# The down projection of a decoder layer as seven products of quarters, with sums kept in DRAM

## The chip, the cores and the metric

The kernel runs on one core of one Trainium2 chip. The metric is the device time of one execution in microseconds; the number reported is the median of several runs. A core has the tensor engine (PE, with its weight loads shown apart as PEld), the vector engine (DVE), the scalar engine (ACT), GpSimd (POOL), and the sync engine (SP), whose queue issues every DMA of this kernel. Each engine takes its own instructions in the order in which the program wrote them, and waits at an instruction until what it needs is there.

## What is computed

One layer of a hybrid decoder: a mixing block, a layer norm, a SwiGLU block and a second layer norm, in float32. The change lies in the SwiGLU block and what follows it:

```python
def swiglu(h, w_ffn_in, w_ffn_out):
    gate, up = jnp.split(jnp.einsum('bld,df->blf', h, w_ffn_in), 2, axis=-1)
    return jnp.einsum('blf,fd->bld', jax.nn.silu(gate) * up, w_ffn_out)

xp = layernorm(ALPHA * xp + swiglu(xp, ...), ln2_g, ln2_b)
```

There are 1024 prompt tokens and 32 sample tokens, 1056 in all; the model is 1024 wide, and the hidden layer is 2816 wide, which is 22 tiles of 128 (`NF`).

## The kernel before

Activations are kept transposed: the features lie on the 128 partitions, the tokens run along the row. A float32 product is made of three matmuls. Each operand is split into a high half in a short float format (a copy by ACT) and the remainder (a subtraction by DVE); the three are high by high, high by low and low by high. The splits of weights are lines L183 and L184 in `Weights.split`, those of activation rows L1751 and L1752 in `split`. A weight piece is a page of up to four 128x128 blocks; up to eight raw pieces (`NRAW`) are loaded and up to four (`NSPLIT`) are split ahead of the one in use.

The order on the engines comes from the way the program is written out. The main line writes the matmuls, and between groups of them it calls `unit()`, which splits the next weight piece (`W.step()`) and then lets spawned generators (`layernorm`, `hidden` and the like) write a piece of their work (`pump`). Rows live in pages of 128x544 from three pools of 18, 19 and 45; when a page is taken, POOL writes one column of it (L254), and that memset waits until the page's last user is done. `take` takes a page, `give` returns it; `spare(n)` asks whether n are free.

**Gate and up** (`for f in range(NF)`, 22 turns) already are computed as seven products of quarters: the two inputs halves by gate and up on the weights' side, the two halves of the tokens (512 and 544) by the two halves of the input on the other. A turn has the products A11·B11, A12·B21, S2·T2, S3·T3, A22·T4, S1·T1 and S4·B22; POOL makes the sums S1 to S4 of the weights for each turn (L1677 to L1688), and the sums T of the activations were made once before. For f below 12 (`NE`), A11 and A12 are made earlier, and their results are stored and loaded again (`recall`). At the end of a turn the products silu(gate)·up of both halves of the tokens are stored to DRAM: L2002 for the first half, and L2025 for the second, after the product of L2023.

**Down projection and second norm.** The tokens go in three groups, `GT`: 272, 512 and 272. For each group `hidden(g)` loads the 22 tiles of hidden rows from DRAM and splits them. For each of the 8 output tiles of 128 features, 22 inputs by 3 matmuls add up in one PSUM bank:

```python
mm(ps, wh[:, f % 4, :], xh, start=(f == 0), stop=False)
mm(ps, wh[:, f % 4, :], xl, start=False, stop=False)
mm(ps, wl[:, f % 4, :], xh, start=False, stop=(f == NF - 1))
```

These are L2125 to L2127, 1056 of 272 columns and 528 of 512. The weights are loaded and split anew for each group, 144 pieces. DVE adds the bank to the residual, the first norm's output from DRAM (L2134), and POOL adds up the sum over tiles for the mean (L2136). The norm of a group is a generator which is written between the matmuls of the next group. It subtracts the mean, squares, adds up, makes 1/sqrt by an estimate of ACT and a Newton step of DVE, and multiplies. The last group has its own form, `Last`: most of the mean and of the squares is made while the last tiles are still under way (`center`, L2066 to L2071), and `finish` (L2073 to L2109) corrects this by the last tile and writes the result.

Of the kernel before, what the change touches and what calls it, by code (L numbers as in the profile page):

```python
# [91 lines left out]
GT = [(0, 272), (272, 784), (784, 1056)]  # L92
# [8 lines left out]
HLAG = 3  # L101


class Weights:
# [4 lines left out]
    def __init__(self, k):  # L109
# [5 lines left out]
        self.keep, self.again = {}, {}  # L115

    def raw(self, ap, uses=1):
        self.src.append(ap)
        self.uses.append(uses)
        return len(self.src) - 1  # L120
# [32 lines left out]
    def load(self, upto=1 << 30):  # L153
        while self.loaded < min(upto, len(self.src)) and self.live < NRAW:
            ap = self.src[self.loaded]
            t = self.k.wp.tile([P, 512], F32, tag="wr", bufs=NRAW, name=f"wr{self.loaded}")[:, :ap.shape[1]]
            self.k.nc.sync.dma_start(out=t, in_=ap)
            self.tile[self.loaded] = t
            self.loaded += 1
            self.live += 1  # L160

# [10 lines left out]
    def split(self):  # L172
# [7 lines left out]
        hi, lo = (k.wp.tile([P, 512], F32R, tag=t, bufs=NSPLIT, name=f"{t}{i}")[:, :w] for t in ("wh", "wl"))  # L180
# [53 lines left out]
def _program(k):  # L234
# [1425 lines left out]
    hd = [k.dp.tile([P, T], F32, name=f"hd{f}") for f in range(NF)]  # L1660
# [56 lines left out]
    wfo = I["w_ffo_t"]  # L1717
    fo = {(g, d): W.whole(wfo[:, d * NF * P:(d + 1) * NF * P]) for g in range(len(GT)) for d in range(8)}

# [160 lines left out]
    def hidden(g):  # L1880

        t0, t1 = GT[g]
        w = t1 - t0
        raws = []
        for f in range(NF + HLAG):
            if f < NF:
                yield from wait(("h", f))
                while not spare(3 if ("h", NF - 2) in flags else 11):
                    yield BLOCK
                r = take([P, w], F32, f"hr{g}_{f}")  # L1890
                dma(out=r, in_=hd[f][:, t0:t1])
                raws.append(r)
                if w < 300:
                    x = take([P, HW_], F32R, f"hx{g}_{f}")
                    HL[g, f] = x[:, 0:w], x[:, 272:272 + w]
                else:
                    HL[g, f] = tuple(take([P, w], F32R, f"h{x}{g}_{f}") for x in "xy")
            if f >= HLAG:
                split(*HL[g, f - HLAG], raws[f - HLAG])
                give(f"hr{g}_{f - HLAG}")  # L1900
                flags.add(("hl", g, f - HLAG))
                if f % 2:
                    yield 0.0

    def rows(g):

        t0, t1 = GT[g]
        while not spare(8):
# [330 lines left out]
```

## Time and profile before

| | |
|---|---|
| three runs | 1274.58, 1272.57, 1274.81 us; median 1274.58 |
| the profiled execution | 1276.04 us, span 1274.3 us |
| mean granted clock of the tensor engine | 0.992 |
| moved by DMA | 221.23 MB, mean 174 GB/s |

The runs time the whole execution. The span reaches from the first to the last instruction of the profiled one. In rows of busy time the number behind an x is the count of instructions. "a, b" behind a bar are the busy time in us of the group and the mean of one in ns, and behind a second bar stand the idle time just ahead and what ended it. In rows of waits the three numbers are the total in us, the count and the longest. In a timeline, the first two numbers are start and duration in us. A span of a matmul in such rows overlaps that of its neighbours.

### The profile page before, as it was taken

The page shows a single profiled execution, that of the slowest core. Times are in us where ns is not written, and L with a number is a line of the kernel's source. Part 1 is how long each engine was busy: PE and PEld are TensorE (multiplying, and loading weights), DVE is VectorE, ACT ScalarE, POOL GpSimd, SP SyncE. Part 2 cuts the span into 40 slices and gives each one's busy share as a digit, 9 for nine tenths or more (in the row PEclk, how much of TensorE's full clock was granted, in tenths as well). Part 3 has the DMA queues.
Part 4 walks back from the last instruction along what each step waited for, and adds up shares of the span by engine and source line. Part 5 has one row for each costly group of instructions (what it writes and reads, how often), then busy time and mean ns, then how long its engine had stood idle before and what let it go on. Part 6 is the DMA issues. An engine that isn't in the chain of part 4 may idle for free.

```text
span 1274.3 us, 25095 instructions
## 1 busy us (share of the span) xinstructions
PE 1242.6 (98%) x8679; PEld 1125.3 (88%) x8679; DVE 822.3 (65%) x1845; ACT 585.1 (46%) x1310; POOL 376.6 (30%) x1201
## 2 busy tenths in 40 slices
PE   9999999989999999998999999999999999999996
PEld 7887789989899889986999999889999899888996
DVE  6697974676675675778566566655655775533786
ACT  7674743755646432686222222222423554422664
POOL 1007511206631144515433442233232112111220
PEclk9999999999999999998999999999999999999998
DMA  9986563455435877565544433342323886533671
GB/s 342 311 278 217 170 223 88 154 172 150 124 108 185 293 240 228 182 194 187 166 149 138 151 128 119 107 134 84 108 88 109 272 286 192 162 93 100 206 242 63
DMA packets 146751, 221.23 MB, mean 174 GB/s; under 512 B 23344, under 2 KB 53168, under 8 KB 146608
## 3 DMA queue, kind: packets, MB, share of 16 engines
q1 hardware_dynamic: 146624, 219.63, 53.9%
q8 instruction: 68, 1.11, 0.4%
q14 instruction: 59, 0.48, 0.1%
HBM read 156.30 MB, written 64.29 MB: 173 GB/s over the span
## 4 chain that ended last, share of the span: by engine, by line
PE 58%; DVE 2%; DMA 2%; ACT 1%; issue 1%; POOL 0%; SPq 0%; DVEq 0%; ACTq 0%; POOLq 0%
PE acc L2127 6%; PE acc L1863 6%; PE acc L2125 6%; PE acc L2126 6%; PE acc L1865 6%; PE acc L1864 6%; PE ms L1863 5%; PE ms L1865 5%; PE ms L1864 5%; PE acc L460 2%; PE acc L459 2%; PE acc L458 2%; DMA hr<-hd 1%; PE ms L1459 1%; ACT mx L1584 0%
## 5 line engine op out<-in xcount | busy, mean ns | idle before, releaser
L184 DVE TENSOR_TENSOR wl<-wr,wh 128x512 fp32r<-128x512 f32 (+1 forms) x270 | 191.8, 712 | 116.0 <-ACT wh L183 103.5
L183 ACT CAST wh<-wr 128x512 fp32r<-128x512 f32 (+1 forms) x270 | 161.2, 600 | 225.9 <-PE acc L2126 97.0
L458 PE MATMUL acc<-xh,wh 128*128 128x272 f32 (+1 forms) x528 | 174.8, 331 | 0.0
L460 PE MATMUL acc<-xh,wl 128*128 128x272 f32 (+1 forms) x528 | 174.5, 331 | 0.0
L2127 PE MATMUL acc<-hx,wl 128*128 128x272 f32 (+1 forms) x528 | 171.7, 325 | 2.0 <-DVE wl L184 1.9
L459 PE MATMUL acc<-xl,wh 128*128 128x272 f32 (+1 forms) x528 | 172.3, 327 | 0.1
L2125 PE MATMUL acc<-hx,wh 128*128 128x272 f32 (+1 forms) x528 | 171.3, 324 | 0.2 <-ACT wh L183 0.2
L183 ACT CAST wh<-S 128x512 fp32r<-128x512 f32 x88 | 54.6, 620 | 176.1 <-PE acc L1864 105.9
L2127 PEld LDWEIGHTS acc<-hx,wl 128*128 128x128 f32 x528 | 99.3, 188 | 11.7 <-DVE wl L184 3.8
L458 PEld LDWEIGHTS acc<-xh,wh 128*128 128x128 f32 x528 | 100.7, 191 | 7.8 <-issue 1.2
L459 PEld LDWEIGHTS acc<-xl,wh 128*128 128x128 f32 x528 | 100.4, 190 | 7.8 <-issue 0.8
L2125 PEld LDWEIGHTS acc<-hx,wh 128*128 128x128 f32 x528 | 99.2, 188 | 8.7 <-issue 0.5
L460 PEld LDWEIGHTS acc<-xh,wl 128*128 128x128 f32 x528 | 100.5, 190 | 6.9 <-issue 0.2
L2126 PE MATMUL acc<-hx,wh 128*128 128x272 f32 x352 | 101.3, 288 | 0.2 <-DVE hx L1752 0.2
L184 DVE TENSOR_TENSOR wl<-S,wh 128x512 fp32r<-128x512 f32 x88 | 72.7, 826 | 39.1 <-ACT wh L183 37.3
L2126 PE MATMUL acc<-hy,wh 128*128 128x512 f32 x176 | 69.2, 393 | 0.0
L2126 PEld LDWEIGHTS acc<-hx,wh 128*128 128x128 f32 x352 | 66.3, 188 | 0.7 <-DVE hx L1752 0.5
L460 PE MATMUL acc<-mh,wl 128*128 128x272 f32 (+1 forms) x192 | 62.8, 328 | 0.0
L458 PE MATMUL acc<-mh,wh 128*128 128x272 f32 (+1 forms) x192 | 62.2, 326 | 0.0
L459 PE MATMUL acc<-ml,wh 128*128 128x272 f32 (+1 forms) x192 | 62.1, 324 | 0.0
L1863 PE MATMUL ms<-T2h,wh 128*128 128x272 f32 x176 | 50.8, 290 | 4.0 <-ACT wh L183 4.0
L2136 POOL TENSOR_TENSOR s<-y,s 128x272 f32<-128x272 f32 (+1 forms) x17 | 22.5, 1324 | 102.1 <-DVE y L2134 102.0
(649 smaller groups left out, 3439.3 us busy)
## 6 DMA issues: line engine op xcount, KB each, us to landing
wr<-in_w_ffo_t SPq DMA_DIRECT2D x120, 256.0 KB, 2.8
wr<-in_w_ffi_t SPq DMA_DIRECT2D x112, 256.0 KB, 2.7
wkh<-wh SPq DMA_DIRECT2D x60, 256.0 KB, 4.3
wkl<-wl SPq DMA_DIRECT2D x60, 256.0 KB, 4.1
wh<-wkh SPq DMA_DIRECT2D x60, 256.0 KB, 3.2
wl<-wkl SPq DMA_DIRECT2D x60, 256.0 KB, 3.6
wr<-in_w_in_t SPq DMA_DIRECT2D x44, 256.0 KB, 5.3
hd<-x SPq DMA_DIRECT2D x22, 272.0 KB, 2.5
```

Of the source, the lines that this page charges most:

```text
L183: nc.scalar.copy(hi, raw)
L184: nc.vector.tensor_tensor(lo, raw, hi.bitcast(F32), ALU.subtract)
L458: mm(ps[:, :cw], wh, xh[kt][:, c0:c0 + cw], start=(kt == 0), stop=False)
L459: mm(ps[:, :cw], wh, xl[kt][:, c0:c0 + cw], start=False, stop=False)
L460: mm(ps[:, :cw], wl, xh[kt][:, c0:c0 + cw], start=False, stop=(kt == n - 1))
L1863: mm(o, wh[:, kt, :], xh, start=(start and kt == 0), stop=False, **kw)
L1864: mm(o, wh[:, kt, :], xl, start=False, stop=False, **kw)
L1865: mm(o, wl[:, kt, :], xh, start=False, stop=(kt == 3), **kw)
L2125: mm(ps, wh[:, f % 4, :], xh, start=(f == 0), stop=False)
L2126: mm(ps, wh[:, f % 4, :], xl, start=False, stop=False)
L2127: mm(ps, wl[:, f % 4, :], xh, start=False, stop=(f == NF - 1))
L2136: G.tensor_tensor(ssum, t, ssum if d > 1 else tiles[0], ALU.add)
```

## The change

The down projection is written as seven products too. The 22 hidden tiles fall into two halves of 11 (`HALF1`, `HALF2`), the 8 output tiles into 0 to 3 and 4 to 7, the tokens into 512 and 544. The products, in this order, are A11·B11, A12·B21, S2·T2, S3·T3, A22·T4, S1·T1, S4·B22. Each is made for four output tiles, of 11 inputs by 3 matmuls each. B11, B21 and T4 are 512 wide; T2, T3, T1 and B22 are 544 wide and take twice 272. S4·B22 is made for one half of 272 tokens after the other, and its 12 split weight pieces stay in pages in between (`Kept`).

- `h_sums` makes T1 to T4 from the hidden rows of two turns on DVE, at the end of each turn whose f is in `HALF2`, and stores them beside B11, B21, B22. The rows x1 and x2 of the turn in `HALF1` are held until then.
- `weight_sums` loads the four quarters of the down weights, in 12 groups (8 of 512 columns, 4 of 384), makes S1 to S4 on POOL and stores them. It is spawned at the end of turn 2 (`WSUM`). Its quarters are loaded in 64 pieces.
- `hidden` loads and splits 77 rows, seven times 11, in the order of the products; it begins at the end of turn 17 as before, once `weight_sums` is through.
- The weights come in 84 pieces of 512 or 384 columns, those of the sums from what was stored.
- Results add up in the pages of the residual (`Y`) and in four pages `x1s`. The norm of the first 512 tokens is spawned after A22·T4, that of the next 272 after the first half of S4·B22, and `Last` does the last 272.

```diff
-GT = [(0, 272), (272, 784), (784, 1056)]
+NJ = 11
+HALF1 = [0, 1, 4, 5, 8, 9, 12, 13, 16, 17, 20]
+HALF2 = [2, 3, 6, 7, 10, 11, 14, 15, 18, 19, 21]
+WSUM = 2
...
+    DOWN = [("A11", "B11"), ("A12", "B21"), ("S2", "T2"), ("S3", "T3"), ("A22", "T4"), ("S1", "T1"), ("S4", "B22")]
+    WD = {n: 512 if n in ("B11", "B21", "T4") else HW_ for _, n in DOWN}
+    GRP = [(0, 4), (4, 8), (8, NJ)]
...
+    def weight_sums():
+        for d in range(4):
+            for g, (a, b) in enumerate(GRP):
+                while not spare(12):
+                    yield BLOCK
+                w = (b - a) * P
+                t = {n: take([P, w], F32, f"d{n}") for n in ("A21", "A22", "A11", "A12")}
+                for n in t:
+                    W.fetch(t[n], down_block(n, d, g))
+                s1, s2 = (take([P, w], F32, f"d{n}") for n in ("S1", "S2"))
+                yield from idle(3)
+                G.tensor_tensor(s1, t["A21"], t["A22"], ALU.add)
...
+                G.tensor_tensor(t["A12"], t["A12"], s2, ALU.subtract)
+                dma(out=sd["S4"][d][g], in_=t["A12"])
+                give("dA12", "dS2")
+                yield 0.0
+        flags.add("wsums")
...
+    def h_sums(j, b11, b12, b21, b22):
+        f1, f2 = HALF1[j], HALF2[j]
+        while not spare(2):
+            yield BLOCK
+        t2 = take([P, HW_], F32, f"ht2_{j}")
+        V.tensor_tensor(b11[:, 0:512], b12[:, 0:512], b11[:, 0:512], ALU.subtract)
+        A.copy(b11[:, 512:HW_], b12[:, 512:HW_])
+        dma(out=hd["T1"][j], in_=b11)
+        yield 0.0
+        V.tensor_tensor(t2, b22, b11, ALU.subtract)
+        dma(out=hd["T2"][j], in_=t2)
+        give(f"x2_{f1}")
+        yield 0.0
+        V.tensor_tensor(b12, b22, b12, ALU.subtract)
+        dma(out=hd["T3"][j], in_=b12)
+        give(f"x1_{f1}", f"x1_{f2}")
+        yield 0.0
+        V.tensor_tensor(b21[:, 0:512], b21[:, 0:512], t2[:, 0:512], ALU.subtract)
+        dma(out=hd["T4"][j], in_=b21[:, 0:512])
+        give(f"x2_{f2}", f"ht2_{j}")
+        for n in ("T1", "T2", "T3", "T4"):
+            flags.add(("t", n, j))
+        yield 0.0
...
-        dma(out=hd[f][:, 512:T], in_=x1)
-        give(f"x1_{f}")
-        flags.add(("h", f))
+        if f in HALF2:
+            dma(out=hd["B22"][j], in_=x1)
+            flags.add(("t", "B22", j))
+            b12, b11, _ = X[HALF1[j]]
+            spawn(h_sums(j, b11, b12, x2, x1))
+        if f == WSUM:
+            spawn(weight_sums())
         if f == NF - HLEAD:
+            need(lambda: "wsums" in flags)
+            spawn(hidden())
...
-    for g, (t0, t1) in enumerate(GT):
+    def down(n, b, d, pss, start=True):
+        for g, (j0, j1) in enumerate(GRP):
+            i = dn[n] + 3 * d + g
+            if i in Kept:
+                wh, wl = Kept[i]
+            else:
+                (wh, wl), = W.begin(i)
+                if n == "S4":
+                    Kept[i] = wh, wl
+            for ps, c0, c1 in pss:
+                o = ps[:, :c1 - c0]
+                for j in range(j0, j1):
+                    need(lambda: ("hl", b, j) in flags)
+                    xh, xl = (x[:, c0:c1] for x in HL[b, j])
+                    kw = {} if start else {"skip_group_check": True}
+                    mm(o, wh[:, j - j0, :], xh, start=(start and j == 0), stop=False, **kw)
+                    mm(o, wh[:, j - j0, :], xl, start=False, stop=False, **kw)
+                    mm(o, wl[:, j - j0, :], xh, start=False, stop=(j == NJ - 1), **kw)
+                    if d == 3 and c1 == WD[b]:
+                        give(f"hx{b}_{j}", f"hy{b}_{j}")
+                    if (j - j0) % 2 and (j - j0 == 1 or c1 - c0 == 512):
+                        unit()
...
+        down("A11", "B11", d, a[d])
+        evac(a[d], lambda ps, c: A.copy(x1s[d][:, c], ps))
...
+        down("A12", "B21", d, a[d], start=False)
+        evac(a[d], lambda ps, c: V.scalar_tensor_tensor(Y[0, d], Y[0, d], ALPHA, ps, ALU.mult, ALU.add))
...
+        down("S2", "T2", d, q)
+        evac(q, lambda ps, c: accumulate(x1s[d], ps, c))
...
+        V.scalar_tensor_tensor(Y[1, d], Y[1, d], ALPHA, x1s[d], ALU.mult, ALU.add)
...
+        down("S3", "T3", d, q)
...
+        evac(q, lambda ps, c: accumulate(x1, ps, c))
...
+        for h, w in ((0, 512), (1, HW_)):
+            V.scalar_tensor_tensor(Y[h, 4 + d], Y[h, 4 + d], ALPHA, x1[:, 0:w], ALU.mult, ALU.add)
...
+        down("A22", "T4", d, q)
+        evac(q, lambda ps, c: accumulate(Y[0, 4 + d], ps, c))
...
+    spawn(layernorm([Y[0, i] for i in range(8)], sm1, 512, 2, "l20", finished(0, "y0_{}"), (LAGM, LAGV), bk="ms",
+                    fine=True))
...
+        down("S1", "T1", d, q)
+        evac(q, lambda ps, c: accumulate(Y[1, 4 + d], ps, c))
+        evac(q, lambda ps, c: accumulate(Y[1, d], ps, c))
...
+    last = Last(sm2[1], 272)
+    for i, c in enumerate(hs2):
+        if not i:
+            spawn(last.center(t2[1]))
+        for d in range(4):
+            q = [(bank("acc"), c.start, c.stop)]
+            down("S4", "B22", d, q)
+            evac(q, lambda ps, c: accumulate(Y[1, d], ps, c))
+            if not i or d < 3:
+                add_up(sm2[i], t2[i], 4 + d)
+            if i:
+                flags.add(("tile", 4 + d))
+        if not i:
+            spawn(layernorm([Y[1, j][:, c] for j in range(8)], sm2[0], 272, 2, "l21", finished(512, None),
+                            (LAGM, LAGV), bk="ms", fine=True))
+    last.finish(t2[1], finished(784, None))
...
```

The order on PE at the start of the down projection, before; `hx` are high halves of hidden rows, `wh` and `wl` the halves of a weight piece, `acc` a PSUM bank:

```order
L2125 MATMUL acc_12766<-hx0_3_11776,wh274_12649 128x272
L2126 MATMUL acc_12766<-hx0_3_11776,wh274_12649 128x272
L2127 MATMUL acc_12766<-hx0_3_11776,wl274_12650 128x272
L2125 MATMUL acc_12766<-hx0_4_11804,wh275_12678 128x272
L2126 MATMUL acc_12766<-hx0_4_11804,wh275_12678 128x272
L2127 MATMUL acc_12766<-hx0_4_11804,wl275_12679 128x272
```

The same place after (`hxB11` and `hyB11` are the halves of rows of B11):

```order
L2233 MATMUL acc_13331<-hxB11_3_12563,wh274_13136 128x512
L2234 MATMUL acc_13331<-hyB11_3_12565,wh274_13136 128x512
L2235 MATMUL acc_13331<-hxB11_3_12563,wl274_13137 128x512
L2233 MATMUL acc_13331<-hxB11_4_12795,wh275_13184 128x512
L2234 MATMUL acc_13331<-hyB11_4_12797,wh275_13184 128x512
L2235 MATMUL acc_13331<-hxB11_4_12795,wl275_13185 128x512
```

A matmul at the start spans 512 tokens where it spanned 272, and a piece of weights goes to one bank in both.

On POOL in a turn of gate and up (names with a number and `wr` belong to the sums of gate and up), before:

```order
L254 MEMSET S1_6_9171 128x1
L1677 TENSOR_TENSOR S1_6_9171<-wr109_8866,wr110_8896 128x512
L1688 TENSOR_TENSOR S2_5_8996<-wr107_8778,S2_5_8996 128x512
L254 MEMSET S2_6_9173 128x1
L1678 TENSOR_TENSOR S2_6_9173<-S1_6_9171,wr108_8864 128x512
L254 MEMSET x3_5_9195 128x1
L254 MEMSET S3_6_9211 128x1
L1682 TENSOR_TENSOR S3_6_9211<-wr108_8864,wr109_8866 128x512
```

After; `dS1`, `dA21` and so on are the pages of `weight_sums`:

```order
L271 MEMSET S1_6_9365 128x1
L1699 TENSOR_TENSOR S1_6_9365<-wr109_8992,wr110_9028 128x512
L271 MEMSET S2_6_9367 128x1
L1700 TENSOR_TENSOR S2_6_9367<-S1_6_9365,wr108_8990 128x512
L1777 TENSOR_TENSOR dS1_9271<-dA21_9255,dA22_9257 128x384
L1781 TENSOR_TENSOR dS2_9273<-dS1_9271,dA11_9259 128x384
L1785 TENSOR_TENSOR dA21_9255<-dA11_9259,dA21_9255 128x384
L271 MEMSET x3_5_9393 128x1
L271 MEMSET S3_7_9625 128x1
L1789 TENSOR_TENSOR dA12_9261<-dA12_9261,dS2_9273 128x384
L271 MEMSET S3_6_9409 128x1
```

Four sums and stores of the down weights now stand between the sums of one turn, ahead of the page for `x3` in which the same turn collects its product, and with them in POOL's order their waits for loads and stores.

On DVE behind the last matmul, before (L2134 is the last add out of PSUM; the rows `last_` and `y2_` belong to the last group's norm):

```order
L2134 SCALAR_TENSOR_TENSOR y2_7_14925<-y2_7_14925,acc_15750 128x272
L2076 TENSOR_TENSOR last_x7_15845<-y2_7_14925,last_c_15680 128x272
L2079 TENSOR_TENSOR last_c_15680<-ms_15688,last_c_15680 128x272
L2084 TENSOR_TENSOR y2_0_14904<-y2_0_14904,last_c_15680 128x272
L2087 SCALAR_TENSOR_TENSOR last_q_15682<-ms_15689,last_sq_15684 128x272
L2084 TENSOR_TENSOR y2_1_14907<-y2_1_14907,last_c_15680 128x272
L2084 TENSOR_TENSOR y2_2_14910<-y2_2_14910,last_c_15680 128x272
L2084 TENSOR_TENSOR y2_3_14913<-y2_3_14913,last_c_15680 128x272
L2091 TENSOR_TENSOR last_q_15682<-last_q_15682,last_y_15686 128x272
L2084 TENSOR_TENSOR y2_4_14916<-y2_4_14916,last_c_15680 128x272
L2093 SCALAR_TENSOR_TENSOR last_q_15682<-last_q_15682,last_y_15686 128x272
L2084 TENSOR_TENSOR y2_5_14919<-y2_5_14919,last_c_15680 128x272
```

After, some four rows behind the last add out of PSUM (L1591 to L1593 are the Newton step of the norm of the first 272 tokens of the half, L1600 its product with 1/sqrt; L2190 to L2197 belong to the last 272):

```order
L1591 TENSOR_TENSOR l21vs_16046<-l21vs_16046,l21y_16048 128x272
L2190 TENSOR_TENSOR y1_4_14471<-y1_4_14471,last_c_15716 128x272
L1592 SCALAR_TENSOR_TENSOR l21vs_16046<-l21vs_16046,l21y_16048 128x272
L2193 SCALAR_TENSOR_TENSOR last_q_15718<-ms_15725,last_sq_15720 128x272
L2190 TENSOR_TENSOR y1_5_14474<-y1_5_14474,last_c_15716 128x272
L2190 TENSOR_TENSOR y1_6_14477<-y1_6_14477,last_c_15716 128x272
L2190 TENSOR_TENSOR y1_7_14480<-y1_7_14480,last_c_15716 128x272
L1593 SCALAR_TENSOR_TENSOR l21y_16048<-l21vs_16046,l21y_16048 128x272
L2197 TENSOR_TENSOR last_q_15718<-last_q_15718,last_y_15722 128x272
L2190 TENSOR_TENSOR y1_0_13706<-y1_0_13706,last_c_15716 128x272
L1600 TENSOR_TENSOR y1_0_13706<-y1_0_13706,l21y_16048 128x272
```

Seven more rows of L1600 follow at once, one for each output tile, and then the last group's step L2199 (L2093 before): steps of two norms now alternate there.

More of the change, by code (lines that the diff above doesn't have):

```diff
@@ L1878, in _program, with hidden @@
     HL = {}
-    def hidden(g):
-        t0, t1 = GT[g]
-        w = t1 - t0
+    def hidden():
         raws = []
[L1885 to L1888, printed above, removed]
+        todo = [(n, j) for _, n in DOWN for j in range(NJ)]
+        tags = ("xs", "xp", "hp")
+        for i in range(len(todo) + HLAG):
+            if i < len(todo):
+                n, j = todo[i]
+                yield from wait(("t", n, j))
+                while not spare(HFREE):
@@ L1898, in hidden @@
[L1898 to L1902, printed above, removed]
-                    yield 0.0
-    def rows(g):
-        t0, t1 = GT[g]
-        while not spare(8):
-            assert pump(), "no progress"
-        out = []
-        for d in range(8):
-            out.append(take([P, t1 - t0], F32, f"y{g}_{d}"))
-            dma(out=out[d], in_=yd[d][:, t0:t1])
-        return out
+                HL[n, j] = tuple(take([P, w], F32R, f"h{x}{n}_{j}", tags) for x in "xy")
@@ L1916, in _program, with rows @@
+    def rows(h, ds):
+        t0, w = SG[h]
+        for d in ds:
+            while not spare(1):
+                assert pump(), "no progress"
+            Y[h, d] = take([P, w], F32, f"y{h}_{d}", ("xs", "xp", "hp"))
+            dma(out=Y[h, d], in_=yd[d][:, t0:t0 + w])
+    Y = {}
     X = {}
@@ L2048, in center @@
             self.mean, self.var = bank()[:, :cw], bank()[:, :cw]
-            assert ("tile6",) not in flags
+            assert ("tile", 4) not in flags
             mm(self.mean, ones_r.bitcast(F32), self.ssum, start=True, stop=True)
-            A.activation(self.c, self.mean, AF.Copy, scale=8.0 / 6.0)
+            A.activation(self.c, self.mean, AF.Copy, scale=8.0 / 4.0)
             yield 0.0
-            for i in range(6):
+            for i in range(7):
+                if i > 3:
+                    yield from wait(("tile", i))
                 self.take(i, tiles[i])
                 yield 0.0
-            while ("tile6",) not in flags:
-                yield BLOCK
-            self.take(6, tiles[6])
-            yield 0.0
             yield 0.0
@@ new lines, in _program, with accumulate, add_up, tile_from @@
+    Kept = {}
+    def accumulate(t, ps, c):
+        V.tensor_tensor(t[:, c], t[:, c], ps, ALU.add)
+    def add_up(sm, ts, i):
+        if i:
+            G.tensor_tensor(sm, ts[i], sm if i > 1 else ts[0], ALU.add)
+    def tile_from(h, d, c=slice(0, HW_)):
+        return Y[h, d][:, c]
+    rows(0, range(4))
+    a = []
+    x1s, x3s = [], []
+    for d in range(4):
+        while not spare(1):
+            assert pump(), "no progress"
+        x1s.append(take([P, HW_], F32, f"dx1_{d}"))
+        G.memset(x1s[d][:, 512:HW_], 0.0)
+        a.append(banks("acc", 512))
+        down("A11", "B11", d, a[d])
+        evac(a[d], lambda ps, c: A.copy(x1s[d][:, c], ps))
@@ new lines, in _program @@
+    rows(1, range(4))
+    need(lambda: room("hp", 3))
+    sm1 = page([P, 512], F32, "s20")
+    for d in range(4):
+        down("A12", "B21", d, a[d], start=False)
+        evac(a[d], lambda ps, c: V.scalar_tensor_tensor(Y[0, d], Y[0, d], ALPHA, ps, ALU.mult, ALU.add))
+        drop("acc")
+        add_up(sm1, [Y[0, i] for i in range(d + 1)], d)
+    rows(0, range(4, 8))
+    for d in range(4):
+        q = banks("ms", HW_)
+        down("S2", "T2", d, q)
+        evac(q, lambda ps, c: accumulate(x1s[d], ps, c))
+        drop("ms", 2)
+        V.scalar_tensor_tensor(Y[1, d], Y[1, d], ALPHA, x1s[d], ALU.mult, ALU.add)
@@ new lines, in finished, with done @@
+    def finished(t0, last):
+        def done(i, t):
+            dma(out=O["yT"][i, :, t0:t0 + t.shape[1]], in_=t)
+            if last:
+                give(last.format(i))
+        return done
+    spawn(layernorm([Y[0, i] for i in range(8)], sm1, 512, 2, "l20", finished(0, "y0_{}"), (LAGM, LAGV), bk="ms",
+                    fine=True))
+    sm2 = []
+    for i in range(2):
+        need(lambda: room("hp"))
+        sm2.append(page([P, 272], F32, f"s2{i + 1}"))
+    hs2 = [slice(0, 272), slice(272, HW_)]
```

164 lines of the change are left out of this document (97 added, 67 removed).

## Prediction

> **What bounds the kernel now.** I read the page first, for engines and the chain that ended last, then who waits on PE, then the matmuls of the down stage one by one, and last the stretch in which the new work lies.
>
> ```profile
> span 1274.3 us, 25095 instructions
> PE 1242.6 (98%) x8679; PEld 1125.3 (88%) x8679; DVE 822.3 (65%) x1845; ACT 585.1 (46%) x1310; POOL 376.6 (30%) x1201
> ...
> PE 58%; DVE 2%; DMA 2%; ACT 1%; issue 1%; POOL 0%; SPq 0%; DVEq 0%; ACTq 0%; POOLq 0%
> ```
>
> The tensor engine PE holds the chain, and DVE, ACT and POOL have room. The waits of PE from the start of the down stage to the end, all that the view lists:
>
> ```profile
> PE acc L2127 <- DVE wl L184: 1.9, 5, 0.6
> PE acc L2126 <- DVE hx L1752: 0.2, 1, 0.2
> PE ms L2078 <- ACT last_q L2077: 0.2, 1, 0.2
> PE acc L2125 <- ACT wh L183: 0.2, 1, 0.2
> ```
>
> About 2.5 us: a matmul less here is time off the span. What one is worth is its spacing, since records overlap. The timeline of PE (start, duration):
>
> ```profile
> 995.10 0.29 PE L2125 MATMUL acc<-hx,wh 128*128 128x272 f32 x1
> ...
> 1060.06 0.29 PE L2125 MATMUL acc<-hx,wh 128*128 128x272 f32 x1
> ...
> 1065.05 0.29 PE L2126 MATMUL acc<-hx,wh 128*128 128x272 f32 x1
> ...
> 1068.67 0.40 PE L2125 MATMUL acc<-hx,wh 128*128 128x512 f32 x1
> ...
> 1074.21 0.39 PE L2125 MATMUL acc<-hx,wh 128*128 128x512 f32 x1
> ...
> 1260.49 0.28 PE L2127 MATMUL acc<-hx,wl 128*128 128x272 f32 x1
> ```
>
> Between the second and third row are 40 steps: 4.99 / 40 = 0.1248 us for one of 272 columns. Between the fourth and fifth are 24: 5.54 / 24 = 0.2308 us for one of 512. The down stage lasts from 995.1 to 1260.6, 265.5 us; its 1056 short and 528 long matmuls make 253.7, 24 matmuls of the last gate turn that run in between make 3.0, and 8.8 us are lost to its start and the layer norms' sums on PE.
>
> **The matmuls.** After: three products of 512 columns and four of twice 272, each 4 output tiles by 11 inputs by 3 matmuls: 396 long and 1056 short ones. The short ones are as many as before; 132 long ones go: 132 x 0.2308 = **-30.5 us**. Nothing hides them, as the waits above show.
>
> **The down stage's helpers.** What must keep pace with PE there, by shape:
>
> ```profile
> L184 DVE TENSOR_TENSOR wl<-wr,wh 128x512 fp32r<-128x512 f32 x118 | 86.1, 733 | 71.9 <-ACT wh L183 68.7 <-DMA wr<-in_w_ffo_t 2.5
> L1752 DVE TENSOR_TENSOR hy<-hr,hx 128x512 fp32r<-128x512 f32 x22 | 15.0, 685 | 8.9 <-ACT hx L1751 8.9
> ...
> L2134 DVE SCALAR_TENSOR_TENSOR y<-y,acc 128x272 f32<-128x272 f32 x16 | 6.9, 430 | 1.6 <-PE acc L2127 1.6
> ...
> L1543 DVE TENSOR_TENSOR y<-y,ms 128x512 f32<-128x512 f32 x8 | 5.4, 678 | 0.0
> ```
>
> Weight splits fall from 144 (24 of them of 256 columns) to 84 (28 of 384); splits of the hidden rows rise from 66, 44 of them of 272 columns, to 77 of 512 or 544. On DVE that is 84 x 0.73 + 77 x 0.70 = 115 us at most, beside 28 us of adds (40 of 272 columns by the third row, 4 of 512 and 12 with the residual by the last) and, at 24 instructions for each of the two norms that PE covers, 16 + 10 us of layer norm: 169 of the 223 us that the matmuls take. It fits on the whole. It is tight in two places: the last turns of gate and up, where the order puts 13 hidden splits and 7 weight splits into one turn (0.7 x 20 = 14 us and 11 adds more, some 19 of 20), and the product S1, where the first half's norm is written between the splits. Before lost 8.8 us in this stage for like reasons. I take the same loss after, **0**; bounds are -8.8, if none is left, and +10, half a turn of DVE late.
>
> **The new sums during gate and up.** A turn has 96 short matmuls and 12 long (14.8 us) up to f = 11, whose A11 and A12 were made ahead, and 36 long (20.3 us) from f = 12. In the order the 48 weight sums stand between f = 3 and f = 11: nine turns, 133 us. Such nine turns before, with two saturated stretches (us; busy of PE, PEld, DVE, ACT, POOL; clock; DMA share; GB/s):
>
> ```profile
> 0.00:100.00 100.00, 98.72 (x498) 81.42 (x499) 74.97 (x220) 71.12 (x175) 10.03 (x101) 1.00 0.89 305
> 633.00:766.00 133.00, 133.00 (x975) 128.28 (x974) 83.58 (x144) 32.84 (x54) 55.40 (x100) 1.00 0.43 139
> 1000.00:1040.00 40.00, 38.02 (x286) 35.98 (x285) 33.80 (x58) 27.79 (x52) 6.20 (x37) 1.00 0.92 305
> ```
>
> POOL in that stretch:
>
> ```profile
> L1678 POOL TENSOR_TENSOR S<-S,wr 128x512 f32<-128x512 f32 x10 | 14.9, 1493 | 0.8
> L1677 POOL TENSOR_TENSOR S<-wr,wr 128x512 f32<-128x512 f32 x9 | 12.0, 1339 | 0.7
> L1688 POOL TENSOR_TENSOR S<-wr,S 128x512 f32<-128x512 f32 x9 | 11.7, 1300 | 3.8 <-DVE wl L184 3.8
> L1682 POOL TENSOR_TENSOR S<-wr,wr 128x512 f32<-128x512 f32 x9 | 11.6, 1294 | 0.7
> L254 POOL MEMSET x<- 128x1 f32 x36 | 3.5, 98 | 40.7 <-DVE wl L184 32.7 <-DVE x L2023 7.9
> L254 POOL MEMSET S<- 128x1 f32 x27 | 2.7, 99 | 31.0 <-DMA hd<-x 25.7 <-DVE wl L184 5.4
> ```
>
> - POOL: 37 sums took 50.2 us, 1.36 each. 32 new ones of 512 columns and 16 of 384 (estimate: three quarters) are 60 us, 72 more page memsets 7: 55.4 + 67 = 122 of 133 us.
> - DMA: 139 GB/s x 133 us = 18.5 MB. Added: 11.5 MB of quarters in, 11.5 MB of sums out, and 3.7 MB more of hidden rows (1.90 MB a pair of turns where 1.08 were): 45.2 MB. At the 305 GB/s of the two saturated rows that takes 148 us, 15 more than PE needs. The page's slices of 32 us hold one faster, the first:
>
> ```profile
> GB/s 342 311 278 217 170 223 88 154 172 150 124 108 185 293 240 228 182 194 187 166 149 138 151 128 119 107 134 84 108 88 109 272 286 192 162 93 100 206 242 63
> ```
>
>  At 342 it is 132 us, no lack.
> - SP issues all of these in one queue. A weight load that waits there for POOL to free its buffer, as a store of a sum will, holds all behind it. SP's longest wait in these nine turns:
>
> ```profile
> SPq L157 <- POOL S L1688: 38.4, 9, 5.5
> ```
>
>  Loads are issued up to eight raw pieces, two turns, ahead, and POOL makes S1 to S3 about a turn before PE wants them, so a delay of 10 to 15 us can be swallowed once. Pages are not so far ahead: POOL's memset of a page for x3 stands behind weight sums that wait for their quarters, and DVE's add out of PSUM waits for that page.
> - DVE: 4 differences for each pair of turns:
>
> ```profile
> L2000 DVE TENSOR_TENSOR x<-x,x 128x512 f32<-128x512 f32 x21 | 14.3, 682 | 0.0
> L2023 DVE TENSOR_TENSOR x<-x,x 128x544 f32<-128x544 f32 x21 | 15.1, 720 | 0.1
> ```
>
>  2 x 0.68 + 2 x 0.72 = 2.8 us, 13 us in the nine turns, 97 of 133. Hidden; the fourth waits for the store of its own input, which DVE's queue then feels too.
>
> So three queues stand close to full for 133 us. Bounds for what reaches PE: 0, all swallowed, as no wait of PE is seen in this stretch before; and 15, DMA's whole lack (beyond that see the first rival). The row nearest in kind is 1000 to 1040, with DMA at 0.92 and DVE at 33.8 of 40: PE lost 2.0 of 40 us there, one twentieth, which of 133 is **+7 us**.
>
> **POOL against DVE.** DVE is slowed while POOL reads:
>
> ```profile
> 810.75 1.27 POOL L1677 TENSOR_TENSOR S<-wr,wr 128x512 f32<-128x512 f32 x1
> 810.89 0.44 DVE L1970 TENSOR_TENSOR x<-x,ms 128x272 f32<-128x272 f32 x1 [0.38 <-PE ms L1865]
> 811.40 1.16 DVE L184 TENSOR_TENSOR wl<-S,wh 128x512 fp32r<-128x512 f32 x1
> ```
>
> The add out of PSUM kept its 0.44 us, the split of two SBUF inputs took 1.16 where 0.69 is usual: it ends about one split after POOL did. Over the gate turns the splits from S averaged
>
> ```profile
> L184 DVE TENSOR_TENSOR wl<-S,wh 128x512 fp32r<-128x512 f32 x87 | 72.0, 828 | 39.1 <-ACT wh L183 37.3
> ```
>
> 828 ns against 685, 12.4 us for 84 sums, 0.15 for each; 48 more are 7 us, and DVE at 104 of 133 still has room. The Trainium skill (SBUF — State Buffer, section "Who interferes with whom") has it that a DVE instruction with two SBUF inputs and a GpSimd one that reads SBUF exclude each other for the whole instruction. The 1.16 us row agrees. What this rule does at its fullest is the third rival.
>
> **The tail.** The last half tile's norm is as before, but the half before it now has only 4 x 33 short matmuls (16.5 us) behind it, where it had 528 (66 us). In the order, DVE's rows after the last add out of PSUM hold 12 more: the first half's variance, three Newton steps and eight products; PE has one sum more.
>
> ```profile
> 1260.81 0.44 DVE L2134 SCALAR_TENSOR_TENSOR y<-y,acc 128x272 f32<-128x272 f32 x1 [1.58 <-PE acc L2127]
> 1267.38 2.20 DVE L2100 TENSOR_TENSOR y<-y,last_y 128x272 f32<-128x272 f32 x6
> 1270.30 0.42 DVE L2104 TENSOR_SCALAR y<-y,cols 128x272 f32<-128x272 f32 x1
> ```
>
> Six in 2.20 us are 0.35 apart: 12 x 0.35 = 4.2, and **+4.7 us** with PE's sum at 0.5. DVE is busy without a break from 1262 to 1270.7, so nothing hides them; bounds are 2 (part finds earlier gaps) and 8 (stores of both halves meet).
>
> **The sum.** -30.5 + 0 + 7 + 4.7 = -18.8. The profiled execution took 1276.04 us for its span of 1274.3; 1276.0 - 18.8 = 1257.2. It lies 1.5 above the median of the three runs shown, 1274.58, so the forecast is **1256 us**, 1.5% faster.
>
> **Rivals.**
> 1. Slower: DMA and POOL starve each other in the nine turns. POOL waits for quarters, SP for POOL's stores, weight loads for SP. For it: 122 of 133 us on POOL, with 78 us of waits in order in the same stretch before, which do not all shrink. Against: the lead of two turns. It decides when the stretch grows by 25.8 us (30.5 - 4.7), to 159 us, or 285 GB/s. At 250 GB/s it takes 181: +48, so 1274.6 - 25.8 + 48 = 1297.
> 2. All of the new work stays hidden: 1274.6 - 25.8 = 1249. For it: PE's waits are nil there and queues run ahead. Against: 340 GB/s wanted over 133 us, 305 seen over 100. The Trainium skill (DMA: Bandwidth & Descriptors, section "Where 436 GB/s comes from") gives about 358 GB/s as what HBM leaves one core; 45.2 MB would then take 126 us, an estimate from that page, under 133. No run here shows that rate.
> 3. POOL's sums each shut DVE out for their whole length: 60 + 97 = 157 of 133 us, +24, so 1273, about as before. It is the page's lock at its fullest. Against: 0.15 us for each in the row above, since most of DVE's work there reads PSUM.
> 4. The down stage's start and S1 run at DVE's pace: +10 on the forecast, 1266. For it: 19 of 20 us on DVE in the last turn, and 2 of 40 lost at this place before. Against: B11's rows are split there for one of four output tiles only, and serve the other three.
>
> **How the numbers follow.** A difference under 0.2%, 2.5 us, can't be told from none here. Forecast (1251 to 1262) 0.40; second rival (1245 to 1251) 0.24; fourth (1262 to 1272) 0.11; third, within 2.5 us of before, 0.08; first 0.17. Faster is the first three, 0.75; same 0.08; slower 0.17. The range reaches from 1245, the second rival with a few of the 8.8 lost us back, to 1275, where the third ends: 0.83 in it. For the faster cases alone it is 1245 to 1269.
>
> **What would show it.** Right: 1452 matmuls in the down stage at 0.125 and 0.231 us; in the nine turns a DMA share near 0.9 and POOL near nine tenths, with some 7 us of PE waits on DVE or ACT there; a tail of 18 to 19 us after the last matmul where 13.7 stood. Wrong: PE waits of over 25 us between f = 3 and f = 12; or none; or waits for hidden tiles in A11, A12 or for the kept pieces of S4.

## The result: 1268.07 us, a third of the gain that was forecast

The changed kernel takes 1268.07 us (median of four runs, 1267.62 to 1268.64), the kernel before 1274.69 (1272.57 to 1275.90). The ratio is 0.995, 95% interval 0.9933 to 0.9967. The time lies in the stated range, but the gain is 6.6 us where 18.6 were forecast. The page of the changed kernel, its span, its busy times and its chain:

```profile
span 1266.3 us, 25157 instructions
PE 1217.9 (96%) x8547; PEld 1104.0 (87%) x8547; DVE 889.7 (70%) x1876; ACT 569.4 (45%) x1276; POOL 451.2 (36%) x1433
...
PE 49%; DMA 5%; POOL 4%; DVE 3%; issue 2%; ACT 0%; SPq 0%; DVEq 0%; POOLq 0%; ACTq 0%
```

PE is busy for 24.7 us less, but the span is only 8.0 us shorter: PE now waits where it did not. POOL stands in the chain with 4%, where it had 0. The timeline of PE says where the down stage begins and ends:

```profile
1017.07 0.40 PE L2233 MATMUL acc<-hxB,wh 128*128 128x512 f32 x1
...
1248.49 0.28 PE L2235 MATMUL acc<-hxB,ls 128*128 128x272 f32 x1
```

| stretch of the profiled execution, us | before | after | difference | forecast |
|---|---|---|---|---|
| start to first matmul of the down stage | 995.1 | 1017.1 | +22.0 | +7 |
| first to last matmul of the down stage | 265.4 | 231.4 | -34.0 | -30.5 |
| last matmul to the end of the span | 13.8 | 17.8 | +4.0 | +4.7 |
| span | 1274.3 | 1266.3 | -8.0 | -18.8 |

All that went wrong lies ahead of the down stage. The waits of PE between 600 and 830 us, where the kernel before had none:

```profile
PE ms L1938 <- DVE x L2113: 7.6, 5, 3.7
PE acc L1940 <- DVE wl L201: 3.7, 1, 3.7
PE ms L1940 <- DVE wl L201: 2.9, 3, 2.2
PE ms L1938 <- ACT wh L200: 2.1, 1, 2.1
```

They sum to 16.3 us. The ends of the turns (the product silu(gate)·up, L2023 before and L2126 after) say how the rest came about: turn 2 ended 2.1 us earlier than before, turn 6 was 4.3 late, turn 8 19.8 and turn 11 23.7; after that the delay stays between 20.9 and 24.2 us up to turn 20. These are the turns in which the 48 weight sums stand. PE's own matmuls say the same: up to 662 us they run 2.1 us ahead of the kernel before, from 835 us on 22.0 behind, so PE loses 24.1 us here. The stretch as a whole and two pieces of 3 us (busy of PE, PEld, DVE, ACT, POOL; granted clock; DMA share; GB/s):

```profile
640.00:820.00 180.00, 163.68 (x1120) 153.99 (x1119) 147.42 (x189) 40.42 (x72) 133.86 (x240) 0.97 0.79 265
732.00:735.00 3.00, 1.32 (x7) 1.32 (x8) 2.92 (x5) 0.00 (x0) 1.00 (x7) 0.84 0.83 257
735.00:738.00 3.00, 3.00 (x17) 3.00 (x17) 0.44 (x1) 0.00 (x0) 2.22 (x3) 0.59 1.05 378
```

Over the stretch neither DMA (0.79) nor POOL (134 of 180 us) is full; in the second piece, with 378 GB/s, DMA is. And a wait can cost more than its length: after PE had stood for 3.7 us up to 733.7, the granted clock was 0.59 in the piece from 735 to 738, and matmuls of 272 columns came 0.226 us apart and not 0.125. From 733.9 to 737.4 that is 1.6 us more. Three such places (near 735, 752 and 803 us, behind waits of 3.7, 2.1 and 3.7 us) make about 5 us, by length times missing clock of their pieces of 2 or 3 us; with the waits 21 of the 24.1. It is not a fixed price: the wait of 2.15 us that ended at 728.0 had no such place behind it (granted clock 1.00 from 728 to 730).

One chain of waits, in the timelines of POOL, DVE and PE:

```profile
727.34 1.45 POOL L1785 TENSOR_TENSOR dA<-dA,dA 128x384 f32<-128x384 f32 x1
728.75 1.28 POOL L1704 TENSOR_TENSOR S<-wr,wr 128x512 f32<-128x512 f32 x1
729.98 0.12 POOL L271 MEMSET x<- 128x1 f32 x2
...
731.16 1.57 POOL L1710 TENSOR_TENSOR S<-wr,S 128x512 f32<-128x512 f32 x1
...
730.10 0.69 DVE L2095 TENSOR_TENSOR x<-x,acc 128x512 f32<-128x512 f32 x1 [2.18 <-POOL x L271]
731.53 1.75 DVE L2097 TENSOR_TENSOR x<-x,x 128x512 f32<-128x512 f32 x1
733.20 0.77 DVE L2113 TENSOR_TENSOR x<-x,ms 128x272 f32<-128x272 f32 x2
...
733.68 0.39 PE L1938 MATMUL ms<-B22h,wh 128*128 128x272 f32 x1 [3.69 <-DVE x L2113]
```

POOL's memset that hands over the page x4 stands behind a sum of the down weights (L1785) and one of the gate's (L1704). DVE's add out of PSUM waits for it; behind that, DVE's product takes 1.75 us where 0.68 is usual, while POOL makes a sum of the gate's (L1710); then come the adds that PE needs before it may add S4·B22 into the same bank. So there are two suspects, a queue place and a slow DVE, and bytes as a third.

### The profile page after: what moved, and what is told of

It is laid out like the page before. It is cut to its first block, busy times and chain, and to the rows that moved or that the text cites. A ratio compares the mean times of both kernels' runs of the same rounds, so it can differ in the third digit from the quotient of the medians.

```text
span 1266.3 us, 25157 instructions
## 1 busy us (share of the span) xinstructions
PE 1217.9 (96%) x8547; PEld 1104.0 (87%) x8547; DVE 889.7 (70%) x1876; ACT 569.4 (45%) x1276; POOL 451.2 (36%) x1433
## 4 chain that ended last, share of the span: by engine, by line
PE 49%; DMA 5%; POOL 4%; DVE 3%; issue 2%; ACT 0%; SPq 0%; DVEq 0%; POOLq 0%; ACTq 0%
PE acc L1938 5%; PE acc L1940 5%; PE acc L1939 5%; PE acc L2235 4%; PE acc L2234 4%; PE acc L2233 4%; PE ms L1938 3%; PE ms L1939 3%; PE ms L1940 3%; DMA dA<-in_w_ffo_t 2%; PE acc L477 2%; PE acc L476 2%; PE acc L475 2%; PE ms L2234 2%; PE ms L2235 2%
## 5 line engine op out<-in xcount | busy, mean ns | idle before, releaser
L200 ACT CAST wh<-wr 128x512 fp32r<-128x512 f32 (+1 forms) x198 | 118.9, 604 | 145.2 <-PE ms L1939 46.5
L201 DVE TENSOR_TENSOR wl<-wr,wh 128x512 fp32r<-128x512 f32 (+1 forms) x198 | 145.1, 735 | 55.1 <-ACT wh L200 45.1
L1938 PE MATMUL ms<-B22h,wh 128*128 128x272 f32 x176 | 51.8, 294 | 7.6 <-DVE x L2113 7.6
L1940 PE MATMUL ms<-T2h,wl 128*128 128x272 f32 x176 | 51.2, 294 | 2.9 <-DVE wl L201 2.9
L1940 PE MATMUL ms<-B22h,wl 128*128 128x272 f32 x176 | 51.3, 291 | 0.0
L1939 PE MATMUL ms<-B22l,wh 128*128 128x272 f32 x176 | 51.2, 291 | 0.0
L1939 PE MATMUL ms<-T2l,wh 128*128 128x272 f32 x176 | 51.2, 292 | 0.0
L2233 PE MATMUL acc<-hxT,wh 128*128 128x272 f32 x176 | 51.0, 290 | 0.0
L2235 PE MATMUL acc<-hxT,wl 128*128 128x272 f32 x176 | 51.0, 290 | 0.0
L1938 PE MATMUL acc<-T3h,wh 128*128 128x272 f32 x176 | 51.0, 290 | 0.0
```

What stands on the lines that cost most here:

```text
L200: nc.scalar.copy(hi, raw)
L201: nc.vector.tensor_tensor(lo, raw, hi.bitcast(F32), ALU.subtract)
L1938: mm(o, wh[:, kt, :], xh, start=(start and kt == 0), stop=False, **kw)
L1939: mm(o, wh[:, kt, :], xl, start=False, stop=False, **kw)
L1940: mm(o, wl[:, kt, :], xh, start=False, stop=(kt == 3), **kw)
L2233: mm(o, wh[:, j - j0, :], xh, start=(start and j == 0), stop=False, **kw)
```

## The experiments

Times are medians in us; the change stands at 1268.1, the kernel before at 1274.0 to 1275.4 in the comparisons. Where kernels of different comparisons lie close together, their ratios to the kernel before decide; the ratio of the change is 0.995 (0.9933 to 0.9967). Where a kernel leaves out or narrows sums, its results are not those of the layer: it only shows what the part costs.

### What the weight sums cost, and which part of them

**Left out.**
```diff
-            spawn(weight_sums())
+            flags.add("wsums")
```

> The changed kernel without the weight sums: neither their loads, nor their 48 sums on POOL, nor their stores; the down stage reads other parts of the down weights in their place, as many bytes. Between the turns f = 2 and f = 11 the changed kernel fell 24 us behind the kernel before. If the weight sums are the cause, 1268 - 24 = 1244 us (1242 to 1248), with no wait of PE between 640 and 820 us. If the differences of hidden rows on DVE cause it, 1262 to 1268.

Measured: 1243.7, ratio 0.9759 (0.9744 to 0.9773). PE is busy for the whole stretch:

```profile
640.00:820.00 180.00, 180.00 (x1275) 170.74 (x1274) 131.39 (x227) 47.40 (x83) 68.89 (x136) 1.00 0.49 160
```

So the weight sums cost 24.4 us, and the differences of hidden rows, which are still in, nothing that PE sees.

**Differences of hidden rows left out.**
```diff
-            spawn(h_sums(j, b11, b12, x2, x1))
...
-                dma(out=r, in_=hd[n][j])
+                dma(out=r, in_=hd[{"T1": "B22", "T2": "B22", "T3": "B22", "T4": "B21"}.get(n, n)][j])
```

> The changed kernel without the differences of hidden rows: 44 subtractions on DVE, 11 small copies on ACT and 44 stores of 256 to 272 KB are gone; the down stage loads the stored B22 and B21 in their place, as many bytes. If DVE is late because of them (four stand in one block behind the product of the turn, 0.7 us each, 1.8 where POOL works): 1256 to 1262. If the weight sums alone are the cause: 1265 to 1268.

Measured: 1266.4, ratio 0.9936 (0.9919 to 0.9954), which overlaps that of the change. Gains of 1.6 us are within what the runs differ by (1264.0 to 1269.0).

**Narrow sums.**
```diff
-                G.tensor_tensor(s1, t["A21"], t["A22"], ALU.add)
+                G.tensor_tensor(s1[:, 0:16], t["A21"][:, 0:16], t["A22"][:, 0:16], ALU.add)
```

> The weight sums with their loads, stores, pages and places in the queues, but 16 columns wide on POOL where they were 512 or 384 (the down stage reads other parts of the down weights). Takes some 60 us of POOL's work away and leaves the 23 MB. Theory POOL (its sums fill its queue, hold back the pages of x3 and x4, and shut DVE out while both read SBUF): most of the 24 us comes back, 1244 to 1252. Theory DMA (the loads come late because the DMA engines are full): 1262 to 1268.

Measured: 1257.2, ratio 0.9857 (0.9832 to 0.9883). Neither theory has it: 11 us come back, 13 stay.

**Narrow loads and stores.**
```diff
-                dma(out=sd["S1"][d][g], in_=s1)
+                dma(out=sd["S1"][d][g][:, 0:32], in_=s1[:, 0:32])
```

The loads are narrowed likewise, to 16 columns, and the sums read four quarters that are loaded once.

> The weight sums at full width on POOL, from four quarters loaded once, with every load and store kept in its place but 16 or 32 columns wide: 22 of the 23 MB are gone, the 48 sums and all issues stay (the down stage reads other parts of the down weights). Theory POOL: 1260 to 1268, waits of PE stay. Theory DMA: most of the 24 us comes back, 1244 to 1252. If each holds part, both this and the narrow sums lie between, and the two gains add to less than that of leaving the sums out.

Measured: 1268.8, nothing back, with DMA at 0.53 over 640 to 830 us. The bytes, on which the forecast had rested its 7 and its 15 us, are not the price.

**Narrow sums, and POOL busy with writing.** Two memsets of the whole page behind each narrow sum, shown against the narrow sums:
```diff
+                for _ in range(2):
+                    G.memset(s1[:, 0:w], 0.0)
```

> As the narrow sums (16 columns), but each followed by two memsets of its whole page, so that POOL is busy about as long as with the sums (some 1.3 us each) and reads next to nothing. Theory occupancy (POOL's time in its queue is what holds back claims and the gate's sums): 1265 to 1270, as the change. Theory lock (DVE's instructions with two SBUF inputs stand still while POOL reads SBUF): as the narrow sums, 1255 to 1259, and DVE's splits of the gate's sums fall from a mean of 1.16 us between 640 and 820 us to about 0.9.

Measured: 1260.6, ratio 0.9897 (0.9880 to 0.9913), between the two expectations. POOL is nearly as busy as with the sums (122 of the 180 us from 640 to 820, 134 in the change), and still the kernel is 7.5 us faster than the change, 3.4 slower than with narrow sums. By the intervals each of the two numbers is good to some 3 us, and what POOL's 12 us less are worth is not told apart from the 7.5. DVE's splits of the gate's sums between 640 and 820 us, before, in the changed kernel, with narrow sums, and with narrow sums and memsets:

```profile
L184 DVE TENSOR_TENSOR wl<-S,wh 128x512 fp32r<-128x512 f32 x46 | 40.3, 877 | 10.4 <-ACT wh L183 9.3
```
```profile
L201 DVE TENSOR_TENSOR wl<-S,wh 128x512 fp32r<-128x512 f32 x40 | 45.3, 1138 | 8.3 <-ACT wh L200 7.7
```
```profile
L201 DVE TENSOR_TENSOR wl<-S,wh 128x512 fp32r<-128x512 f32 x43 | 37.7, 878 | 11.5 <-ACT wh L200 10.6
```
```profile
L201 DVE TENSOR_TENSOR wl<-S,wh 128x512 fp32r<-128x512 f32 x42 | 40.0, 952 | 8.6 <-ACT wh L200 7.5
```

The differences of hidden rows show it more strongly: the 23 in this window took 1.35 us each in the changed kernel and 0.96 with memsets (of their four kinds, one, 1.43 and 1.35, hardly changed). Over the nine turns of the weight sums, from the end of turn 2 to that of turn 11, the busy times (PE, PEld, DVE, ACT, POOL) before, in the changed kernel, without weight sums, and with narrow sums and memsets are:

```profile
655.90:790.20 134.30, 134.30 (x975) 129.08 (x974) 85.27 (x146) 33.44 (x55) 54.55 (x99) 1.00 0.41 132
```
```profile
653.80:813.90 160.10, 143.78 (x989) 135.50 (x988) 130.78 (x166) 34.43 (x62) 126.57 (x223) 0.97 0.84 280
```
```profile
652.70:787.00 134.30, 134.30 (x974) 129.10 (x973) 100.55 (x166) 35.62 (x62) 54.69 (x107) 1.00 0.53 174
```
```profile
655.00:810.30 155.30, 146.43 (x1010) 139.32 (x1010) 105.18 (x166) 35.98 (x64) 114.09 (x321) 0.97 0.88 289
```

With the same 166 instructions DVE is busy for 130.8 us in the change and 100.6 without weight sums: they add 30 us to DVE without giving it a single instruction, and narrow sums with memsets in their place add under 5. It goes both ways: the last two sums of a group of 512 columns took 1.70 and 1.65 us on POOL in the changed kernel, where the gate's took 1.29 to 1.46 in the same window before. The Trainium skill (SBUF — State Buffer, section "Who interferes with whom") says that a DVE instruction with two SBUF inputs contends with a GpSimd instruction that reads SBUF, and not with one that only writes it. The memsets agree, by DVE's 105 us against 131.

**Both narrow.** The narrow loads and stores, with sums 32 columns wide.

> As the kernel with narrow loads and stores, and its sums 32 columns wide too: what is left are the issues, pages and places in the queues, with hardly any bytes and hardly any time on POOL. If the 13 us left with narrow sums are the bytes: 1243 to 1248. If they are the issues, pages and places in the queues: 1254 to 1258.

Measured: 1260.7, ratio 0.9886 (0.9866 to 0.9905), above both expectations. So 17 us stay with almost no bytes and almost no work. What is left is the issues, the pages and the places in the queues; that these cost the 17 us follows from what was taken away, and the waits fit. Why it is more than the 13 of the narrow sums alone is not shown. The waits of DVE between 640 and 830 us:

```profile
DVE x L2090 <- POOL x L271: 9.5, 3, 6.5
```

and of POOL:

```profile
POOL dS L271 <- DMA dA<-in_w_ffo_t: 13.5, 5, 3.7
POOL dA L1790 <- DMA dA<-in_w_ffo_t: 10.5, 8, 3.6
```

POOL, hardly busy with sums (86.5 of 190 us in all), still stands waiting for loads and for pages that loads hold, with the memsets for x3 and x4 behind it.

### The page memsets

**Without them for x3 and x4** (`page` leaves the memset out; DVE then waits for the page itself):
```diff
-        G.memset(t[:, 0:1].bitcast(F32), 0.0)
+        if not name.startswith(("x3_", "x4_")):
+            G.memset(t[:, 0:1].bitcast(F32), 0.0)
```

> The changed kernel without POOL's one-column memset for the pages x3 and x4, so that DVE itself waits for the page's last user and no longer for POOL's place in its queue. Theory claim (DVE's adds out of PSUM stand behind POOL's weight sums through these memsets, and PE behind the adds): 4 to 12 us come back, 1256 to 1264. Theory lock (DVE is slow because POOL reads SBUF at the same time, and the gate's own sums come late): 1266 to 1269.

Measured: 1265.8 (1264.0 to 1271.1), ratio 0.9929 (0.9914 to 0.9945), which overlaps that of the change. Alone it gives 2.3 us, if anything: the waits move to the pages themselves and to the gate's sums.

**The same with narrow sums.**

> The narrow sums, and the pages x3 and x4 without POOL's memset. With narrow sums 13 us were left of the loss, with POOL nearly idle but standing in front of sums whose quarters had not come (30 us of such waits between 640 and 830 us). If the memsets of x3 and x4 queued behind these waits carry the 13 us: 1245 to 1250. If the late loads of the gate's own weights and the pages do: 1255 to 1258.

Measured: 1251.9, ratio 0.9824 (0.9806 to 0.9842), 5.3 us below the narrow sums, 8.2 above no sums at all. The interval overlaps that of the narrow sums a little. It lies between the two expectations: if the difference holds, the memsets carry part of the 13 us, not all, and what carries the other 8 is not shown. Where DVE stood for POOL when it needed the page x3, the profile now puts its longest waits there down to transfers, among them stores of weight sums:

```profile
DVE x L2085 <- DMA wr<-in_w_ffi_t: 5.4, 1, 5.4
DVE x L2085 <- DMA sdS<-dA: 5.2, 2, 3.7
```

### When the sums stand

**Spread.**
```diff
-                yield from idle(3)
+                yield from idle(8)
```

> The same 48 weight sums, with eight idle steps ahead of each group where there were three: they stand between f = 3 and f = 17 instead of f = 3 and f = 11, so the last five groups lie in the long turns of 20.3 us. Nothing else changes. If the loss is a matter of how densely POOL's queue is filled, half or more of the 24 us comes back: 1250 to 1260. If each group costs PE some 2 us wherever it stands, 1265 to 1270.

Measured: 1261.8, ratio 0.9893 (0.9881 to 0.9906), between the two expectations. Only a quarter comes back. DVE's longest wait is a single one for a memset, and two waits make most of PE's 12.2 us:

```profile
DVE x L2095 <- POOL x L271: 10.9, 2, 8.6
```
```profile
PE ms L1938 <- DVE x L2113: 7.8, 4, 4.8
PE acc L1940 <- DVE wl L201: 4.5, 1, 4.5
```

**Spread, without the memsets for x3 and x4.**

> The spread sums and the pages x3 and x4 without POOL's memset together. If both carry a part of their own, 1245 to 1253, below either alone; if the spread already takes away what the claims waited for, the same as the spread within 2 us.

Measured: 1255.2, ratio 0.9837 (0.9824 to 0.9850), 6.7 below the spread alone, clear of its interval. The memsets gave 2.3 us where POOL is crowded and 6.7 where it is less so: the parts do not simply add.

**Quarters loaded one group earlier**, into four more pages:
```diff
+                t, u = nxt, (3 * d + g) % 2
+                if 3 * d + g < 11:
+                    nxt = fetch(*todo[3 * d + g + 1])
```

> The quarters of each group of weight sums are loaded one group earlier, into four more pages. POOL then no longer stands in front of a group whose quarters are still on their way (14 us of such waits between 640 and 830 us). Theory DMA wait: 3 to 8 us come back, 1260 to 1265. Theory POOL busy: nothing, 1266 to 1270, as the narrow loads and stores gave nothing either.

Measured: 1255.9, 12.2 us, more than either theory had. But the sums had also moved: they now ran from 667 to 883 us where they ran from 656 to 811, because pages were short. Hence the control:

**Four pages held unused, quarters loaded as late as in the change.**
```diff
+        for i in range(4):
+            take([P, 512], F32, f"held{i}")
```

> The early loads of the quarters took four more pages, and for lack of pages they also spread the twelve groups over f = 4 to f = 14, where they stood between f = 3 and f = 11. Here four pages are held unused while the sums go on, and the quarters are loaded as late as in the change: the order on POOL shows the groups between f = 4 and f = 14 too. If the earlier loads themselves gave the 12 us, 1263 to 1268; if it was the spreading, 1254 to 1258; the spread sums (f = 3 to f = 17) at 1262 speak for 1260 to 1263 with half of it from each.

Measured: 1252.3 (1251.0 to 1256.7), ratio 0.9833 (0.9811 to 0.9854). The sums run from 663 to 866 us. Without the earlier loads it is no slower than with them (0.9845, 0.9832 to 0.9857). The theory that POOL's wait for late quarters was the cost falls; the gain came with the later and wider places of the sums.

**Earlier loads, without the memsets.**

> Early sums as in the change, with the quarters loaded one group earlier and without POOL's memset for x3 and x4. The two did -12 and -2 us alone. Theory claim (what the memsets wait for is mainly a sum that waits for its quarters): little more than the earlier loads alone, 1253 to 1256. Independent parts: 1250 to 1253.

Measured: 1251.7, ratio 0.9830 (0.9815 to 0.9845). The medians say 4.2 below the earlier loads alone, the ratios 1.9, and the intervals overlap: that the memsets still cost something beside the earlier loads is not shown.

**Late.**
```diff
-WSUM = 2
+WSUM = 9
```

> The same weight sums, three idle steps to a group as in the change, but spawned at the end of turn 9 and not of turn 2: they stand between f = 9 and f = 17, mostly in the long turns of 20.3 us, in which DVE and POOL have more room beside PE. Some 160 us for the twelve groups, as now. If what counts is how closely the groups follow each other, 1264 to 1270. If it is the room that a turn leaves DVE and POOL, 1246 to 1255.

Measured: 1252.9, ratio 0.9839 (0.9818 to 0.9860). The sums run from 752 to 918 us, about as densely as in the change (165 us where it was 155), but mostly in turns of 20.3 us, and 15 us come back. So at the same density places in longer turns give back as much as wider places among the short turns did.

**Late, with earlier loads.**

> The late sums with the quarters loaded one group earlier. If POOL's wait for quarters is a cost of its own, some 3 to 8 us below the late sums alone, down to the 1244 of the kernel without weight sums; if the long turns cover that wait, the same as the late sums within 2 us.

Measured: 1251.4, the same as late alone.

**Late, earlier loads, no memsets for x3 and x4.**

> Late sums (from f = 9 on), quarters loaded one group earlier, and no memset of POOL for x3 and x4, all three. Late sums alone gave 1253, the kernel without weight sums 1244. If the rest of 9 us is still POOL's queue, 1246 to 1250; if it is the lock between DVE and POOL, which none of the three takes away, 1250 to 1253.

Measured: 1248.0 (1244.9 to 1251.9), ratio 0.9785 (0.9767 to 0.9803). It computes all that the reference does, and is the fastest of those that do, 20 us below the change and 26 below the kernel before. The median is what was expected if the rest was POOL's queue; the runs reach into the other expectation too. 4.3 us over the kernel without weight sums are left. Its profiled execution was the longest of the four, so its trace does not settle where they lie.

## Why the forecast was wrong, step by step

**The matmuls: right.** -30.5 forecast. 396 long and 1056 short matmuls stand in the stage, and at 0.2308 and 0.1248 us they make 223.2 where 253.7 stood.

**The down stage's helpers: right, on the good side.** Zero was taken, bounds -8.8 and +10. The stage became 34.0 shorter, 3.5 more than the matmuls. Less the matmuls of the stage and the 24 of the gate that run in between (3.0 us), 8.7 us were lost before and 5.2 after. The fourth rival, a start at DVE's pace, did not come: one wait of PE from 1010 us to the end is all there is.

```profile
PE acc L2235 <- DVE wl L201: 1.7, 1, 1.7
```

**The tail: right.** +4.7 forecast, +4.0 measured. The first half's norm stands in it as the order had it:

```profile
1254.52 2.89 DVE L1600 TENSOR_TENSOR y<-y,l21y 128x272 f32<-128x272 f32 x8
```

**The new sums during gate and up: the step that failed.** +7 forecast, bounds 0 and 15; +22 at the start of the down stage. The step had priced the sums by how full DMA is: 45.2 MB at 305 GB/s as the upper bound, and the share lost in a stretch with DMA at 0.92 as the value. Taking the bytes away gave nothing back (1268.8), so this was the price of the wrong thing. What the runs showed in its place:
- The weight sums cost 24.4 us in all. Their width on POOL makes 11 of these with all else in place, of which some 7 go when POOL writes for nearly as long without reading (DVE kept waiting by POOL's reads) and the rest, some 3, fits POOL's time.
- 13 stay with narrow sums, and 17 with narrow sums and narrow transfers: issues, pages and places in queues. The memsets for x3 and x4 behind them carry some 5 of the 13, if the overlapping intervals allow it; the other 8 are open. Loading the quarters earlier gave nothing that later and wider places alone did not give.
- Three of PE's four waits of over 2 us were followed by some 3.5 us at a granted clock of 0.50 to 0.59, about 5 us in all, a term that the sum did not have.

**POOL against DVE: mis-sized.** It was taken at 0.15 us for each of 48 sums, 7 us of DVE's time and none of PE's; the third rival was held to be unlikely "since most of DVE's work there reads PSUM". In the nine turns DVE was busy for 130.8 us where 104 were expected. The differences of hidden rows made 15 of what was added (13 forecast), the weight sums 30 (7 forecast), 0.63 us for each sum. The splits, products and differences have two SBUF inputs, single ones took up to 1.8 us, and they stand ahead of the adds that PE waits for. So the price taken from turns with one kind of sum did not carry over to turns with more than twice as many.

**The rivals.** The first, that POOL and SP hold each other up, had the mechanism nearest to what happened (waits in order, not bytes), but named DMA's rate as its price and a loss of 48 us; its wait for quarters was not the cost either, by the earlier loads. It would have decided from 25.8 us on; 22 came, so the change is still faster. The third, POOL's sums shutting DVE out, was a part of some 7 us and not 24. In the same nine turns, 160.1 us long where 134.3 stood, the signs named beforehand read so: PE waits of 16.3 us where 7 were expected, POOL at 127 of 160 and not at nine tenths, DMA at 0.84 and not at 0.9. The amounts of work were right (POOL 127 us where 122 were forecast, 280 GB/s over 160.1 us where 45.2 MB were). None of the three queues was full over the turns, and PE waited all the same.

What stays open: why spreading over 250 us (1261.8) gave less than over 200 us (1252.3). The traces say where: with the sums spread, two waits of PE, 4.8 and 4.5 us, each with a place of low granted clock, make 9.3 of its 12.2 us; with four pages held no wait is over 1.9 us (8.3 in all) and no such place is seen. Why the long ones arise is not shown. Each edit also moves POOL's rows in the order, so single stalls come and go; differences of 2 to 4 us between these kernels are not explained one by one.

## What to carry to other kernels

An in-order engine that hands over buffers is part of every chain that takes one. Before work is put there, ask what stands behind each wait of it, and how much longer its neighbour's instructions become, not only how many microseconds it is busy; here 48 sums on a POOL busy for three quarters of the time cost 24 us of the span, with DMA at 0.8. Put such work into the stretch in which its neighbours have most room (moving it seven turns later gave 15 us back), and reckon that a wait of PE of some 2 us or more can cost 1.6 us on top of its length, as three of four did here.

## What was not expected of the hardware

After three of the four waits of 2 to 4 us, PE ran at a granted clock of 0.50 to 0.59 for about 3.5 us: matmuls of 272 columns 0.226 us apart instead of 0.125. The wait of 0.9 us at 664 us cost only itself, and so did that of 2.15 us up to 728.0: the matmuls behind them came at 0.125. The Trainium skill (TensorE: Matmul & The Clock Gate, section "Part 1: The HAM clock gate (the "warmup" mystery)") has the clock halved after an idle window of about 3.4 us, and full again after about 3.4 us of work. With the second 733.9 to 737.4 agrees; the first was not needed here, as a wait of 2.1 us (up to 750.4) was followed by the low clock from 751.1 on. DMA moved 378 GB/s over the 3 us from 735 on, above the 342 that the slices of 32 us of the page had shown before.
